# Forget rows' log sums in the gate stage, residual rows one chunk later, and six other moves in a hybrid decoder layer

## Chip, cores and metric

The kernel runs on one core of a Trainium2 chip. Its time is the device time of one execution in microseconds. The core's engines work in parallel, each through its own queue in order: TensorE (PE, with its weight loads PEld), VectorE (DVE), ScalarE (ACT), GpSimd (POOL) and SyncE (SP), which issues most DMAs.

## What is computed

The reference is one decoder layer for 1024 tokens of width 1024, in float32. Cut to what matters:

```python
z = h @ w_in
hq, hf, hi, hg, sq, sk, sv, mq, gl = split_cols(z, IN_SPLITS)
f = lb + (1 - lb) * sigmoid(hf); k = 1 - f
b = cumsum(log f) within chunks of 64 tokens      # gated recurrence, 8 heads
q_in, k_in, k_out = hq * exp(b), k * exp(-b), k * exp(b_last - b)
o_a = rms_norm(recurrence(q_in, k_in, k_out, hi)) * gain * silu(hg)
o_b = sliding_window_attention(sq, sk, sv)        # 16 heads, window 128
o_c = memory_attention(mq, mem @ w_mem_kv)        # 4 heads, 256 memory rows
merged = sum of sigmoid(gl_i) * (o_i @ w_branch_i)
h = layer_norm(alpha * h + merged @ w_out)
h = layer_norm(alpha * h + relu(h @ w_up) ** 2 @ w_down)
```

## The kernel before

A float32 product is made of three matmuls: each operand is split into a high part (float32r, copied by ScalarE, `L76`) and a low part (the difference, on GpSimd or VectorE, `L77`). A weight tile of 128x1024 is loaded into a tile R, and its two parts go to a tile W; both rings have 4 tiles, S has 2, G and T have 4.

Parts of the layer are computed by a scheme with seven block products in place of eight (Strassen's in Winograd's form): `prod(o, w, g, j)` is twelve matmuls of block product j with the operand `xs[j]`, and `combine` makes the operands 3 to 7 from the four blocks of x. The order in time:

- The keys and values of the memory (to 56 us in the profile), which use the S tiles.
- The gate stage: 16 rows (pairs of weight tiles) that need only x: the two other branch gates, the forget gate hf and the output gate hg. `two` makes products 1 and 2 of the first twelve rows ("the firsts"); meanwhile `x_rest(k)`, k = 0 to 3, makes the operands 3 to 7. Then `run` makes products 6, 4, 7, 5 and 3 of each row (3 is put off into the next row); rows 12 to 15 make all seven. `prepare` loads and combines the weights of a row on GpSimd: w2 (products 4 and 5), w4 (6), w3 (7 and 3). `z_emit` and `z_first` pass the sums through Tanh and store them in `d_z`.
- For each half of the tokens: sliding window attention (`swa_phase`), memory attention (`mem_head`), the recurrence (`hg_head`), output projection, LayerNorm. `hg_gates` loads forget rows and makes Ln, running sums (scans) and Exp in the midst of memory attention.
- The up projection, again by block products, whose operands `flip_h1` turns with TensorE and combines; behind it the down projection, in chunks c of 7 products whose partial sums `pa[j]` stay in SBUF; last, the rows of the output, four products each, with LayerNorm (`last_rows`, `norm_rows`).

Tiles come from rings: a new tile waits until the oldest user of its place is done. Engines take their instructions in the order that the tile framework has laid out, which is not always that of the code; so a change of a ring or of the code moves instructions on all engines.

Of the kernel before, what the change touches and what calls it, by code (L numbers as in the profile page):

```python
# [8 lines left out]
F32 = mybir.dt.float32  # L9
# [6 lines left out]
P = 128  # L16
D = 1024
# [18 lines left out]
def hybrid_layer(ctx: ExitStack, tc: tile.TileContext, a: dict, out: bass.AP):  # L36
# [110 lines left out]
    gainh = const("gainh", [P, 8])  # L147
    d_bias = dr.tile([16, 256], F32, name="d_bias")
# [5 lines left out]
    d_z = dr.tile([16, 4, P, TH], F32, name="d_z")  # L154
    d_g1 = dr.tile([EARLY_Z, P, TH], F32, name="d_g1")
# [39 lines left out]
    def combine(left, right, part, eng):  # L195
# [78 lines left out]
    nc.vector.tensor_scalar(out=c1, in0=lb, scalar1=-0.5, scalar2=0.5, op0=ALU.mult, op1=ALU.add)  # L274
    nc.vector.tensor_scalar(out=gainh, in0=gain, scalar1=0.5, scalar2=None, op0=ALU.mult)
# [60 lines left out]
    def prepare(src0, src1, first):  # L336
# [10 lines left out]
        w4 = st("S", [P, 2, TH], F32R)  # L347
        split(w4[:, 0], w4[:, 1], r1[:, H], nc.vector)
# [3 lines left out]
    def run(ws, p1, held, emit):  # L352
# [17 lines left out]
        b_ = pt("t")  # L370
        prod(b_, w2, 0, 5)
# [8 lines left out]
    zrows = [("w_gate", 0), ("w_gate", 16), ("w_hf", 0), ("w_hg", 0)]  # L380
# [6 lines left out]
    def forget(f, h):  # L387
        nc.vector.tensor_scalar(out=f, in0=f, scalar1=1.0, scalar2=c1[:, h:h + 1], op0=ALU.add, op1=ALU.mult)
        nc.vector.tensor_scalar(out=f, in0=f, scalar1=lb[:, h:h + 1], scalar2=None, op0=ALU.add)

    def z_emit(i):
        box = []

        def emit(b, o, s_):
# [4 lines left out]
            if i < 12:  # L399
# [121 lines left out]
    def swa_phase(hf, x, merged, fill_last):  # L521
# [17 lines left out]
        nc.scalar.copy(vt, o)  # L539
# [755 lines left out]
```

## Time and profile before

| | us |
|---|---|
| median of 3 runs (lowest, highest) | 2166.62 (2166.34, 2167.66) |
| profiled execution | 2166.51 |
| its span, first to last instruction | 2164.7 |
| TensorE busy | 2054.9 (95%) |
| VectorE, GpSimd, ScalarE busy | 1252.5, 959.3, 837.7 |

The span is what the profile shows between the first and the last instruction. An engine's busy time counts its instructions and not its waits; TensorE's busy time is longer where the granted clock was lower (mean 0.983 of full speed).

### The profile page before, as it was taken

Reading aid. Unit: us, or ns where it says so; the run is one execution under the profiler, and the core shown is the slowest. Engines: PE = TensorE matmul, PEld = TensorE weight load, DVE = VectorE, ACT = ScalarE, POOL = GpSimd, SP = SyncE. Lnnn points to the kernel's source line nnn. Section 1 sums busy time; section 2 is a strip of 40 time slices with the busy share of each in tenths; the row PEclk is TensorE's granted clock in tenths of the full one; section 3 lists DMA queues with packets and bytes.
Section 4 is the critical chain, followed back from the end, with each engine's and each line's share of the span. In section 5 each row is a group of like instructions: output and inputs, shape, how many; then the busy total and the mean of one; then the engine's idle time right before and its main releaser. Section 6 shows DMA issues by size and latency. Waiting matters only on the chain. (4 is left out here: it accounts for less than half of the span.)

```text
span 2164.7 us, 26923 instructions
## 1 busy us (share of the span) xinstructions
PE 2054.9 (95%) x10050; PEld 1688.5 (78%) x10050; DVE 1252.5 (58%) x2092; ACT 837.7 (39%) x1480; POOL 959.3 (44%) x478
## 2 busy tenths in 40 slices
PE   8969998999999999999999999999899999999996
PEld 8747776777787898877778889887678887788875
DVE  5643276566536346256753624626566656598898
ACT  5423222344335233335433614333544454433322
POOL 2556665421222522751122242274533334777674
PEclk9989999999999999999999999999999999999998
DMA  8653432422233323544123332354657547744322
GB/s 281 215 161 127 155 121 93 145 89 69 60 102 110 124 84 117 177 145 136 59 69 103 102 123 84 121 187 144 199 186 228 182 145 240 275 136 154 116 88 78
DMA packets 125762, 299.30 MB, mean 138 GB/s; under 512 B 11408, under 2 KB 24896, under 8 KB 125632
## 3 DMA queue, kind: packets, MB, share of 16 engines
q1 hardware_dynamic: 124736, 294.42, 41.7%
q10 hardware_dynamic: 896, 3.16, 0.5%
q8 instruction: 79, 1.29, 0.3%
q14 instruction: 51, 0.42, 0.1%
HBM read 232.51 MB, written 65.03 MB: 137 GB/s over the span
## 5 line engine op out<-in xcount | busy, mean ns | idle before, releaser
L77 POOL TENSOR_TENSOR W<-R,W 128x1024 fp32r<-128x1024 f32 x205 | 497.0, 2426 | 879.3 <-ACT W L76 835.1
L61 PE MATMUL pz<-X,W 128*128 128x512 f32 x2016 | 491.9, 398 | 30.5 <-ACT W L76 11.3
L76 ACT CAST W<-R 128x1024 fp32r<-128x1024 f32 (+1 forms) x287 | 293.8, 1024 | 469.5 <-PE pz L61 226.1
L61 PEld LDWEIGHTS pz<-X,W 128*128 128x128 f32 x2016 | 377.7, 191 | 114.4 <-POOL W L77 12.9
L61 PE MATMUL pz<-O,W 128*128 128x512 f32 x1152 | 267.1, 391 | 0.0
L61 PEld LDWEIGHTS pz<-O,W 128*128 128x128 f32 x1152 | 214.9, 188 | 46.2 <-issue 1.5
L61 PE MATMUL pt<-O,W 128*128 128x512 f32 x768 | 188.0, 393 | 2.3 <-DVE T L296 2.3
L61 PEld LDWEIGHTS pt<-O,W 128*128 128x128 f32 x768 | 142.3, 188 | 39.5 <-DVE T L296 10.3
L77 DVE TENSOR_TENSOR W<-R,W 128x1024 fp32r<-128x1024 f32 (+1 forms) x84 | 100.5, 1197 | 75.3 <-ACT W L76 74.9
L61 PE MATMUL pz<-BT,W 128*128 128x512 f32 x384 | 102.1, 419 | 24.8 <-DVE G L315 9.7
L61 PEld LDWEIGHTS pz<-BT,W 128*128 128x128 f32 x384 | 76.4, 203 | 47.6 <-issue 12.7
L61 PE MATMUL ps<-W,BT 128*128 128x512 f32 x360 | 98.4, 391 | 5.3 <-DVE X L296 3.3
L61 PE MATMUL pz<-W,BT 128*128 128x512 f32 x354 | 96.3, 390 | 0.4 <-DVE X L1070 0.4
L61 PE MATMUL pz<-W,X 128*128 128x256 f32 x768 | 95.8, 284 | 0.0
L77 POOL TENSOR_TENSOR BT<-R,BT 128x1024 fp32r<-128x1024 f32 x27 | 72.1, 2671 | 51.4 <-ACT BT L76 51.4
L61 PE MATMUL ps<-X,W 128*128 128x512 f32 x384 | 93.0, 391 | 1.6 <-DVE G L296 1.6
L61 PEld LDWEIGHTS pz<-W,X 128*128 128x128 f32 x768 | 93.1, 192 | 0.0
L61 PE MATMUL ps<-T,W 128*128 128x512 f32 x384 | 92.2, 389 | 0.0
L61 PEld LDWEIGHTS ps<-X,W 128*128 128x128 f32 x384 | 72.6, 189 | 17.5 <-DVE G L296 2.3
L341 POOL TENSOR_TENSOR R<-R,R 128x512 f32<-128x512 f32 x48 | 64.3, 1340 | 48.8 <-DMA R<-in_w_gate_dram 31.1
L61 PEld LDWEIGHTS ps<-T,W 128*128 128x128 f32 x384 | 72.1, 188 | 15.0
L77 POOL TENSOR_TENSOR MG<-R,MG 128x1024 fp32r<-128x1024 f32 (+1 forms) x30 | 79.5, 2651 | 9.0 <-ACT MG L76 9.0
(277 smaller groups left out, 3454.9 us busy)
## 6 DMA issues: line engine op xcount, KB each, us to landing
R<-d_ff SPq DMA_DIRECT2D x49, 512.0 KB, 3.6
R<-in_w_b_dram SPq DMA_DIRECT2D x48, 512.0 KB, 3.5
R<-in_w_up_dram SPq DMA_DIRECT2D x42, 512.0 KB, 4.1
R<-in_w_gate_dram SPq DMA_DIRECT2D x40, 512.0 KB, 3.6
d_ff<-T SPq DMA_DIRECT2D x56, 256.0 KB, 2.8
d_z<-T SPq DMA_DIRECT2D x52, 256.0 KB, 2.0
G<-d_z SPq DMA_DIRECT2D x48, 256.0 KB, 2.8
d_ff<-S SPq DMA_DIRECT2D x48, 256.0 KB, 2.3
```

What stands on the lines that cost most here:

```text
L61: nc.tensor.matmul(o, lhsT=l, rhs=r, start=start, stop=stop, skip_group_check=more)
L76: (hi_copy or nc.scalar.copy)(hi, src)
L77: (lo_eng or nc.gpsimd).tensor_tensor(out=lo, in0=src, in1=f32(hi), op=ALU.subtract)
L341: nc.gpsimd.tensor_tensor(out=o, in0=a_, in1=b_, op=op)
```

## The change

It does eight things. `x_rest` takes its raw tiles from S and not from R, and `prepare(0)` moves behind the firsts; w4 of a row takes a W tile, not S. In the rows with early firsts, products 4 and 5 come ahead of 6 and 7. The rows hf and hg change places, and the forget rows make k = 1 - f, Ln, scans, Exp and the subtraction in the gate stage; k goes to `d_z`, the sums to a new `d_b`, the ends of the chunks stay in `elc`; `hg_gates` only loads. The copy of v in `swa_phase` goes to VectorE. `flip_h1` of half 2 keeps one turned block in PSUM and the left blocks in a tile R; in `combine`, products 6 and 4 change engines. The residual rows are loaded in chunks 1 to 4 of the down projection and added there by five operations of 128x2048. In six of the eight last rows, ScalarE makes sum and squares in place of VectorE's bn_stats.

```diff
@@ x_rest
-            raw = st("R", [P, 2, TH])
+            raw = st("S", [P, 2, TH])
@@ prepare
-        w4 = st("S", [P, 2, TH], F32R)
-        split(w4[:, 0], w4[:, 1], r1[:, H], nc.vector)
+        w4 = st("W", [P, 2, 1024], F32R)
+        split(w4[:, 0, L], w4[:, 1, L], r1[:, H], nc.vector)
@@ combine
-        part(6, b22, 1)
+        part(6, b22, 0)
...
-        part(4, b21, 0)
+        part(4, b21, 1)
@@ run
+        if p1 is not None:
+            c, b_ = four(), five()
         prod(o, w4, 0, 6, p1 is not None)
...
         prod(o, w3, 0, 7, False)
@@ rows
-    zrows = [("w_gate", 0), ("w_gate", 16), ("w_hf", 0), ("w_hg", 0)]
+    zrows = [("w_gate", 0), ("w_gate", 16), ("w_hg", 0), ("w_hf", 0)]
@@ forget, called behind the last addition of rows 12 to 15
+    def forget(i, f, ks):
+        for b in range(4):
+            h = 2 * (i - 12) + b % 2
+            nc.scalar.activation(ks[b // 2][:, b % 2], f[:, b, :], AF.Identity, scale=nc1[:, h:h + 1], bias=c1[:, h:h + 1])
+            nc.sync.dma_start(d_z[i, b], ks[b // 2][:, b % 2])
+            nc.vector.tensor_scalar(out=f[:, b, :], in0=f[:, b, :], scalar1=c1[:, h:h + 1], scalar2=c1b[:, h:h + 1],
+                                    op0=ALU.mult, op1=ALU.add)
+        nc.scalar.activation(f, f, AF.Ln)
+        for b in range(4):
+            nc.vector.tensor_tensor_scan(out=f[:, b, :], data0=reset, data1=f[:, b, :], initial=0.0,
+                                         op0=ALU.mult, op1=ALU.add)
+        h = 2 * (i - 12)
+        nc.scalar.activation(elc[:, h:h + 2, :, :].rearrange("p h f c -> p f h c"),
+                             f.rearrange("p (f h) (c t) -> p f h c t", f=2, t=64)[:, :, :, :, 63], AF.Exp)
+        gp = f.rearrange("p h (c u t) -> p (h c) u t", u=2, t=64)
+        nc.vector.tensor_tensor(out=gp[:, :, 0, :], in0=gp[:, :, 0, :],
+                                in1=gp[:, :, 0, 63:64].broadcast_to([P, 16, 64]), op=ALU.subtract)
+        nc.sync.dma_start(d_b[i - 12].rearrange("b p t -> p b t"), f)
@@ gate stage
-        if i == EARLY_Z - 3:
-            ws = prepare(*zsrc(0), False)
...
-        if i:
-            ws = prepare(*zsrc(i), i >= EARLY_Z)
+        ws = prepare(*zsrc(i), i >= EARLY_Z)
@@ swa_phase
-        nc.scalar.copy(vt, o)
+        nc.vector.tensor_copy(vt, o)
@@ hg_gates (its finish(), with Ln, scans and Exp, is gone)
+        for pp in range(2):
+            i = 2 * b4 + pp
+            nc.sync.dma_start(fk[:, 2 * pp:2 * pp + 2, :], d_z[12 + i, 2 * hf:2 * hf + 2].rearrange("b p t -> p b t"))
+            nc.sync.dma_start(gg[:, 2 * pp:2 * pp + 2, :], d_b[i, 2 * hf:2 * hf + 2].rearrange("b p t -> p b t"))
@@ flip_h1
-            both = st("W", [P, 2, 8, P])
+            left = st("R", [P, 8, P])
...
+                if g == 0:
+                    t = st("G", [P, TH]).rearrange("p (k t) -> p k t", k=4)
+                    nc.scalar.copy(t, o)
+                    o = t
+                right.append(o)
@@ down
-            rows_h1(2, 0, 0)
-            rows_h1(5, 1, 1)
-            rows_h1(3, 0, 1)
-            nc.gpsimd.tensor_tensor(out=pa[3], in0=pa[3], in1=pa[5], op=ALU.subtract)
-            rows_h1(0, 1, 0)
...
-            if c == 0 and j in (2, 3, 5):
-                nc.vector.scalar_tensor_tensor(out=pa[j][:, b, :], in0=pa[j][:, b, :], scalar=ALPHA, in1=o,
-                                               op0=ALU.mult, op1=ALU.add)
+        if 1 <= c <= 4:
+            rows_h1(0, *((1, 0), (0, 0), (0, 1), (1, 1))[c - 1])
...
+                for j, sign in (((4, 1),), ((2, 1),), ((3, 1),), ((5, 1), (3, -1)))[c - 1]:
+                    nc.vector.scalar_tensor_tensor(out=pa[j], in0=pa[0], scalar=sign * ALPHA, in1=pa[j], op0=ALU.mult,
+                                                   op1=ALU.add)
@@ last_rows
+                if own:
+                    nc.vector.bn_stats(out=bn[:, ch, :], in_=v)
+                else:
+                    nc.scalar.activation(st("G", [P, TH]), v, AF.Copy, accum_out=ss[:, ch:ch + 1])
...
+                    nc.scalar.activation(st("G", [P, TH]), parts[ch][0], AF.Square, bias=neg, accum_out=qq[:, ch:ch + 1])
```

How the instructions stand on three engines. GpSimd's queue before, at the end of the firsts: row 34 is the low part of w3 of gate row 0, rows 35 and 36 and rows 39 and 40 begin the combining of rows 1 and 2, rows 37 and 38 are the low parts of the firsts' weights 10 and 11.

```order
34 L77 TENSOR_TENSOR W_1117<-R_1103,W_1117 128x1024 [waits Activation_49]
35 L341 TENSOR_TENSOR R_1264<-R_1264,R_1266 128x512 [waits DMAHW7_49,DMAHW5_49,DVE_49]
36 L341 TENSOR_TENSOR R_1266<-R_1266 128x512 [waits Pool_49]
37 L77 TENSOR_TENSOR W_1122<-R_1120,W_1122 128x1024 [waits DMAHW1_49,Activation_49]
38 L77 TENSOR_TENSOR W_1162<-R_1160,W_1162 128x1024 [waits DMAHW2_49,Activation_49]
39 L341 TENSOR_TENSOR R_1360<-R_1360,R_1362 128x512 [waits DMAHW4_49,DMAHW1_49,Pool_49]
40 L341 TENSOR_TENSOR R_1362<-R_1362 128x512 [waits DMAHW0_49,Pool_49]
41 L77 TENSOR_TENSOR W_1270<-R_1266,W_1270 128x1024 [waits Activation_49]
```

The same place now: rows 28 and 31 are the low parts of weights 10 and 11, rows 30 and 32 the last pieces of x_rest(3), row 34 is w2 of gate row 0, row 38 its w3, and row 33 begins gate row 1.

```order
28 L77 TENSOR_TENSOR W_1111<-R_1109,W_1111 128x1024 [waits Activation_49]
29 L347 TENSOR_TENSOR R_1191<-R_1191 128x512 [waits Pool_49]
30 L77 TENSOR_TENSOR O_116<-S_1051,O_116 128x512 [waits DMAHW1_49,Activation_49]
31 L77 TENSOR_TENSOR W_1151<-R_1149,W_1151 128x1024 [waits Activation_49]
32 L77 TENSOR_TENSOR T_122<-S_1051,T_121 128x512 [waits Activation_49]
33 L347 TENSOR_TENSOR R_1270<-R_1270,R_1272 128x512 [waits DMAHW7_49,DMAHW5_49,Pool_49]
34 L77 TENSOR_TENSOR W_1195<-R_1191,W_1195 128x1024 [waits Activation_49]
35 L347 TENSOR_TENSOR R_1272<-R_1272 128x512 [waits Pool_49]
36 L347 TENSOR_TENSOR R_1191<-R_1191,R_1189 128x512 [waits Pool_49]
37 L347 TENSOR_TENSOR R_1189<-R_1189,R_1191 128x512 [waits Pool_49]
38 L77 TENSOR_TENSOR W_1203<-R_1189,W_1203 128x1024 [waits Activation_49]
39 L347 TENSOR_TENSOR R_1366<-R_1366,R_1368 128x512 [waits DMAHW6_49,DMAHW3_49,DVE_49]
```

So the low parts of the weights 10 and 11 no longer stand behind the combining of gate row 1, but behind x_rest; and the combined weights of row 0 come behind all of it.

VectorE's queue before, between two late gate rows (T_2542 and T_2677 are the sums of two rows; row 225 is a copy that TensorE waits for):

```order
222 L404 SCALAR_TENSOR_TENSOR T_2542<-G_2660,T_2542 128x512 [waits Activation_49]
223 L296 TENSOR_TENSOR T_2677<-ps_2664,G_2645 128x512 [waits DMAHW6_49,DMAHW4_49,DMAHW7_49,DMAHW2_49,PE_49]
224 L404 SCALAR_TENSOR_TENSOR T_2677<-G_2679,T_2677 128x512 [waits Activation_49]
225 L315 COPY G_2695<-pz_2632 128x512 [waits PE_49]
226 L77 TENSOR_TENSOR S_2760<-R_2752,S_2760 128x512 [waits DMAHW5_49,Activation_49]
```

And now (T_2413 is row 12, T_2558 row 13; the rows of L416 are the scans, listed under their opcode's name; row 203 waits for Exp; rows 198 and 204 are copies for TensorE):

```order
198 L321 COPY G_2573<-pz_2494 128x512 [waits PE_49]
199 L416 SCALAR_TENSOR_TENSOR T_2413<-reset,T_2413 128x512 [waits Activation_49]
200 L416 SCALAR_TENSOR_TENSOR T_2413<-reset,T_2413 128x512
201 L416 SCALAR_TENSOR_TENSOR T_2413<-reset,T_2413 128x512 [waits DVE_49]
202 L416 SCALAR_TENSOR_TENSOR T_2413<-reset,T_2413 128x512
203 L422 TENSOR_TENSOR T_2413<-T_2413 128x16x64 [waits Activation_49]
204 L321 COPY G_2600<-pz_2494 128x512 [waits PE_49]
205 L412 TENSOR_SCALAR T_2558<-T_2558,c_76,c1b 128x512 [waits Activation_49]
206 L302 TENSOR_TENSOR T_2558<-ps_2575,G_2600 128x512 [waits DVE_49]
207 L302 TENSOR_TENSOR T_2558<-pt_2604,G_2600 128x512 [waits PE_49]
```

The copy behind product 6 (row 198) is free of the STT; the copy behind product 7 (row 204) now stands behind the scans and the subtraction of the row before.

ScalarE's queue before, at the first flip of the up projection: rows 792 to 798 are the flip's casts, rows 799 and 801 the weights 4 and 5.

```order
792 L76 CAST O_11493<-W_11639 128x4x128 [waits Activation_49]
793 L929 ACTIVATE G_11634<-G_11634 128x512 [waits Activation_49]
794 L76 CAST O_11494<-W_11639 128x4x128 [waits DMAHW4_49,DVE_49]
795 L76 CAST BT_11497<-W_11639 128x4x128 [waits DVE_49]
796 L76 CAST MG_11495<-W_11639 128x4x128 [waits DVE_49]
797 L292 COPY G_11685<-pz_11672 128x512 [waits DMAHW6_49,PE_49]
798 L76 CAST T_11499<-W_11639 128x4x128 [waits DVE_49]
799 L76 CAST W_11775<-R_11773 128x1024 [waits DMAHW2_49,DVE_49,Pool_49]
```

And now: row 802 is weight 5 (weight 4 is row 796), rows 805 to 811 are the flip's casts, two of them from PSUM.

```order
802 L76 CAST W_11824<-R_11822 128x1024 [waits DMAHW1_49,PE_49,Pool_49]
803 L924 COPY G_11656<-pt_11651 128x512 [waits DMAHW2_49,PE_49]
804 L948 ACTIVATE G_11644<-G_11644 128x512 [waits DVE_49]
805 L76 CAST O_11503<-pt_11658 128x4x128 [waits PE_49]
806 L949 ACTIVATE G_11644<-G_11644 128x512 [waits Activation_49]
807 L76 CAST O_11504<-R_11649 128x4x128 [waits DMAHW4_49,DVE_49]
808 L76 CAST BT_11507<-G_11656 128x4x128 [waits DVE_49]
809 L76 CAST MG_11505<-pt_11658 128x4x128 [waits DVE_49]
810 L298 COPY G_11695<-pz_11682 128x512 [waits DVE_49,PE_49]
811 L76 CAST T_11509<-R_11649 128x4x128 [waits DVE_49]
```

Both weights have moved ahead of the flip.

## Rows read from the trace of the kernel before

**Rows 1.** The page: busy time of each engine.

```profile
PE 2054.9 (95%) x10050; PEld 1688.5 (78%) x10050; DVE 1252.5 (58%) x2092; ACT 837.7 (39%) x1480; POOL 959.3 (44%) x478
```

**Rows 2.** What TensorE waits for: microseconds in total, times, the longest.

```profile
PE pz L61 <- POOL W L77: 11.1, 3, 8.8
PE pz L61 <- DVE G L315: 9.7, 3, 3.3
PE ps L61 <- DVE O L99: 5.7, 2, 3.3
PE ps L61 <- ACT BT L98: 4.0, 2, 2.0
```

**Rows 3.** Timeline, TensorE, end of the firsts: start, duration, operation, idle before.

```profile
123.95 1.22 PE L61 MATMUL pz<-X,W 128*128 128x512 f32 x2 [6.75 <-ACT W L76]
133.97 4.64 PE L61 MATMUL pz<-X,W 128*128 128x512 f32 x10 [8.80 <-POOL W L77]
146.90 2.88 PE L61 MATMUL pz<-MG,S 128*128 128x512 f32 x12
```

**Rows 4.** Timeline, VectorE and TensorE, gate row 14, then busy and granted clock.

```profile
388.23 2.41 DVE L404 SCALAR_TENSOR_TENSOR T<-G,T 128x512 f32<-128x512 f32 x1 [3.57 <-ACT G L403]
391.39 4.57 PE L61 MATMUL pz<-BT,W 128*128 128x512 f32 x12 [3.28 <-DVE G L315]
391.50:394.50 3.00, 3.00 (x8) 2.34 (x9) 1.22 (x1) 0.62 (x1) 1.55 (x2) 0.52 0.25 89
```

**Rows 5.** Timeline, VectorE and TensorE, start of half 2.

```profile
963.62 2.14 DVE L1192 TENSOR_TENSOR sm<-sm,sm 128x1 f32<-128x1 f32 x1
968.39 6.88 PE L61 MATMUL pz<-X,W 128*128 128x512 f32 x22 [4.54 <-ACT G L539]
```

**Rows 6.** Timeline, TensorE, up projection.

```profile
1514.23 0.93 PE L61 MATMUL pz<-X,W 128*128 128x512 f32 x2 [4.53 <-ACT W L76]
```

**Rows 7.** Timeline, TensorE, first chunk of the down projection.

```profile
1843.70 2.93 PE L61 MATMUL ps<-W,MG 128*128 128x512 f32 x6 [4.34 <-DVE O L1070]
```

**Rows 8.** Timeline, TensorE's last matmuls and VectorE's last scale.

```profile
2144.30 0.84 PE L61 MATMUL pz<-W,MG 128*128 128x512 f32 x3
2157.92 0.16 DVE L1211 SCALAR_TENSOR_TENSOR sm<-sm,sm 128x1 f32<-128x1 f32 x1
```

**Rows 9.** Timeline, SyncE's queue and VectorE: memory keys' store, loads and end of x_rest.

```profile
65.57 0.33 SPq L253 DMA_DIRECT2D d_mkv<-S  x1
84.06 0.38 SPq L218 DMA_DIRECT2D R<-in_xT_dram  x1
98.82 0.39 SPq L218 DMA_DIRECT2D R<-in_xT_dram  x1
111.45 0.69 DVE L77 TENSOR_TENSOR T<-R,T 128x512 fp32r<-128x512 f32 x1
```

**Rows 10.** Timeline, GpSimd, low parts in the gate loop.

```profile
194.21 2.40 POOL L77 TENSOR_TENSOR W<-R,W 128x1024 fp32r<-128x1024 f32 x1
209.26 2.40 POOL L77 TENSOR_TENSOR W<-R,W 128x1024 fp32r<-128x1024 f32 x1
215.56 2.38 POOL L77 TENSOR_TENSOR W<-R,W 128x1024 fp32r<-128x1024 f32 x1 [1.16 <-ACT W L76]
```

**Rows 11.** Timeline, ScalarE and VectorE, hg_gates of half 1.

```profile
685.08 1.28 ACT L674 ACT_TABLE_LOAD   x1
686.38 1.91 ACT L674 ACTIVATE T<-T 128x2048 f32<-128x2048 f32 x1
659.57 6.34 DVE L677 TENSOR_TENSOR_SCAN T<-reset,T 128x512 f32<-128x512 f32 x4
```

**Rows 12.** VectorE on 128x2048: groups by line, then the timeline.

```profile
L1093 DVE SCALAR_TENSOR_TENSOR X<-X 128x2048 f32<-128x2048 f32 x1 | 2.6, 2567 | 0.0
2096.05 4.49 DVE L296 TENSOR_TENSOR O<-O,O 128x2048 f32<-128x2048 f32 x1
```

**Rows 13.** Stretch of the down projection: busy PE, PEld, DVE, ACT, POOL.

```profile
1880.00:1930.00 50.00, 49.97 (x221) 41.08 (x220) 44.09 (x51) 18.03 (x18) 39.63 (x15) 1.00 0.51 168
```

More of the change, by code (lines that the diff above doesn't have):

```diff
@@ L154, in hybrid_layer @@
     d_z = dr.tile([16, 4, P, TH], F32, name="d_z")
+    d_b = dr.tile([4, 4, P, TH], F32, name="d_b")
     d_g1 = dr.tile([EARLY_Z, P, TH], F32, name="d_g1")
@@ L274, in hybrid_layer @@
     nc.vector.tensor_scalar(out=c1, in0=lb, scalar1=-0.5, scalar2=0.5, op0=ALU.mult, op1=ALU.add)
+    nc.vector.tensor_scalar(out=nc1, in0=c1, scalar1=-1.0, scalar2=None, op0=ALU.mult)
+    nc.vector.tensor_tensor(out=c1b, in0=c1, in1=lb, op=ALU.add)
     nc.vector.tensor_scalar(out=gainh, in0=gain, scalar1=0.5, scalar2=None, op0=ALU.mult)
@@ L362, in run, with four, five @@
             emit(0, d, s1)
+        c, b_ = None, None
+        def four():
+            c_ = pt("s")
+            prod(c_, w2, 1, 4)
+            return c_
+        def five():
+            t = pt("t")
+            prod(t, w2, 0, 5)
+            return t
+        if p1 is not None:
+            c, b_ = four(), five()
         prod(o, w4, 0, 6, p1 is not None)
         s2 = copy_out(o) if p1 is None else plus(o, p1)
-        c = pt("s")
-        prod(c, w2, 1, 4)
+        if p1 is None:
+            c = four()
         prod(o, w3, 0, 7, False)
@@ L369, in run @@
         emit(1, c, s3)
-        b_ = pt("t")
-        prod(b_, w2, 0, 5)
+        if p1 is None:
+            b_ = five()
         emit(3, b_, s3)
@@ L404, in emit @@
                 nc.vector.scalar_tensor_tensor(out=f, in0=th, scalar=1.0, in1=f, op0=ALU.add, op1=ALU.mult)
-            if 8 <= i < 12:
-                forget(f, 2 * (i - 8) + b % 2)
-            nc.sync.dma_start(d_z[i, b], f)
+            if i < 12:
+                nc.sync.dma_start(d_z[i, b], f)
+            elif b == 2:
+                forget(i, box[0], [st("S", [P, 2, TH]) for _ in range(2)])
         return emit
@@ L430, in emit @@
             add(t, o, s_)
-            nc.scalar.activation(t, t, AF.Tanh, scale=0.5)
-            if i >= 8:
-                forget(t, 2 * (i - 8) + b % 2)
+            if i // 4 == 2:
+                u = st("G", [P, TH])
+                nc.scalar.activation(u, t, AF.Tanh, scale=0.5)
+                nc.vector.scalar_tensor_tensor(out=t, in0=u, scalar=1.0, in1=t, op0=ALU.add, op1=ALU.mult)
+            else:
+                nc.scalar.activation(t, t, AF.Tanh, scale=0.5)
             nc.sync.dma_start(d_z[i, b], t)
@@ L800, in hybrid_layer @@
                 hgs = [hg_gates(0, hf)]
-                hgs[0][3]()
         v = keep()
@@ L888, in flip_h1 @@
                 return
-            both = st("W", [P, 2, 8, P])
-            left, right = both[:, 0], both[:, 1]
+            left = st("R", [P, 8, P])
             nc.sync.dma_start(left, d_h1t[:, :, ts])
+            right = []
             for g in range(2):
@@ L1142, in last_rows @@
             bn = sb.tile([P, 4, 6], F32, tag="bn", name=nm("bn"), bufs=8)
+            own = b in (2, 3)
+            ss = small(2)
             parts = []
@@ L1200, in layer_norm, with norm_rows @@
             store(cs, v)
-def norm_rows(nc, small, parts, bn, g, b, eps, mhalf, store, last):
-    mv, e, y, z, nb = small(2), small(1), small(1), small(1), small(1)
-    nc.vector.bn_aggr(out=mv, in_=bn)
+def norm_rows(nc, small, parts, mv, g, b, eps, mhalf, store, last):
+    e, y, z, nb = small(1), small(1), small(1), small(1)
     nc.vector.tensor_scalar(out=e, in0=mv[:, 1:2], scalar1=eps, scalar2=None, op0=ALU.add)
```

77 lines of the change are left out of this document (32 added, 45 removed).

## The prediction

> **What bounds the kernel now.** I read the engine shares first: TensorE is busy for 2054.9 of 2164.7 us [rows 1]. The change leaves the number of matmuls alone, so it can act only on the 110 us in which TensorE stands, and on matmuls at the lower granted clock. Next came the list of what TensorE waits for, then the timeline around each long wait. The waits lie in few places: the gate stage (weights that come late from ScalarE and GpSimd, [rows 2, 3], and copies of VectorE, [rows 2, 4]), the memory attention of both halves (5.7 us behind O of VectorE and 4.0 behind BT of ScalarE, [rows 2]), the start of half 2 [rows 5], of the up projection [rows 6] and of the down projection [rows 7], and the time behind the last matmul [rows 8]. A long wait has a second price: the twelve matmuls behind it take 4.57 us [rows 4] against 2.88 [rows 3], at a granted clock of 0.52, the level of 1.2 GHz [rows 4], so 1.7 us lost. The profiled execution took 2166.51 us, 0.1 below the median of 2166.62; the sum is made against 2166.5.
>
> **Gate start, the largest term.** In the program before, POOL's queue holds the subtraction of gate row 1, which waits for a DMA, ahead of the low parts of weights 10 and 11, so TensorE stood 6.75 and 8.80 us [rows 3] and reached the first product of row 0 at 146.90. Twelve firsts from 56 us need 12 x 5.44 = 65.3 us, so without waits they would end at 121.4. The change orders POOL otherwise, but puts x_rest into the two S tiles. Those belong to the memory keys until the store issued at 65.57 [rows 9] has landed, so the second half of x_rest(0) is issued near 69, my estimate. The chain is as long as before: second halves were issued at 84.06 and 98.82, a cycle of 14.8 us, and the last piece ended at 112.1, 13.3 behind its issue [rows 9]. With two tiles, a load also waits for the chain before it, so I keep 14.8: x_rest(3) is issued near 113.5 and ends near 127. In POOL's new queue the low part of weight 11 stands behind O of x_rest(3) (near 119), so the firsts end near 127, not 121.4. Behind T of x_rest(3) come: sub 1.3, low part of w2(0) 2.4, add 1.3, two subs 2.7, a cast 1.2, low part of w3(0) 2.4, a load 3.7, sub and add 2.6, w2(1) 2.4. That is w2(1) near 147; one POOL row of 15.05 us [rows 10] puts w2(2) at 162 and w2(3) at 177. Before, w2(3) ended at 196.6 [rows 10]: POOL runs 19.5 us earlier.
>
> TensorE does not gain all of it. POOL's row of 15.05 us, against 13.6 us of products, paces the loop before and after; moving products 4 and 5 ahead only moves the short wait that each row has. But the new order places four matmuls of product 4 of row i+1 ahead of product 7 of row i. Before, three products (8.2 us) were left behind the start of w3(11), which is 3.9 us behind the end of w2(11), as in every row [rows 10]; now seven (19.0 us) are left behind w2(11). That costs 19.0 - 12.5 = about 6.5. **Term: -13.** Bounds: if S were free as early as R was, x_rest(3) would end at 112 and the gain be 28; with a cycle 3 us longer it would be 5.
>
> **Late gate rows.** Rows 12 to 15 become the forget rows. Each adds four Identity copies and one Ln of 128x2048 on ScalarE, four small tensor_scalars, four scans and a subtraction on VectorE, five stores. The long ones were measured: Ln 1.91, table load 1.28, scans 6.34 together [rows 11]. They no longer have the STT of 2.41 us ahead of the copy [rows 4], which was behind 9.7 us of waits [rows 2] and three spells of low clock, 14.8 us in all. The new wait: VectorE's subtraction needs ScalarE's Exp, which stands behind a cast that waits for TensorE's product 5. Behind that subtraction stand the copy s3, a tensor_scalar and two additions that TensorE's product 3 needs: four of 0.69 us, as the last row of [rows 9], are 2.8, and 5.7 if those that read SBUF alone are stretched as the STT was. With 2.9 + 1.7 at two borders and 4.4 before the sliding window, where only four matmuls of two weights lie between, the new loss is about 12. **Term: -3** (from -11, all waits gone, to +10).
>
> **Memory attention.** hg_gates now only loads. Gone are the Ln, the scans in front of VectorE's O [rows 11], and the Exp in front of ScalarE's BT: 5.7 + 4.0 + 1.7 = 11.4. I leave 1.9 for new order among the same matmuls; the loads grow from 1 to 2 MB, and VectorE and ScalarE have a whole head's time for them. **Term: -9.5** (-8 to -11).
>
> **Start of half 2.** The copy of v moves from ScalarE, where it stood behind a normalization, to VectorE, behind a small operation that ended at 965.76 [rows 5]; copy 0.69, so TensorE goes on near 966.5 and not 968.39. **Term: -2** (0 to -6 with the clock).
>
> **Up projection.** The turned rows no longer take a weight tile. In ScalarE's new queue the casts of weights 4 and 5 stand ahead of the flip that the cast at the wait of 4.53 us stood behind [rows 6]; that wait goes, and the two behind it that GpSimd ended (2.3, what the list has beside the 8.80, [rows 2]), 6.8 in all, with one spell of 1.7 at least. The waits at row 0 behind them come from GpSimd's low parts, which stay. Cover: two weights (10.9 us of products) between a flip and the weight behind it; a flip's chain took some 7 us. **Term: -8** (-4 to -11).
>
> **Down projection.** The residual leaves chunk 0: no subtraction on GpSimd behind a load, so 4.34 us and the slow matmuls behind it [rows 7] go, and 12 reads of PSUM pass to ScalarE, which is idle half the time. VectorE gets four more STT of 128x2048: 2.57 us each as the one before, 4.49 at worst, as an addition took beside GpSimd [rows 12]. They fall where it is busy 44 of 50 us [rows 13]: one per chunk fits in, two in chunk 4 may not. **Term: -6.5** (-2 to -8.5).
>
> **Last rows.** Two bn_stats per row go from VectorE and four passes with accumulators come to ScalarE, in a loop between both. VectorE ended 12.8 us behind TensorE (2157.92 against 2145.14, [rows 8]). ScalarE has some 5 us of work a row against 5.44 of TensorE, but each row now crosses between the two engines six times. **Term: -0.5** (-4 to +3). Products 6 and 4 changing engines in combine, and the three small constants, cost nothing: VectorE was idle there.
>
> Sum: 13 + 3 + 9.5 + 2 + 8 + 6.5 + 0.5 = 42.5; 2166.5 - 42.5 = **2124**.
>
> **A rule against the change.** In the row, a table load on ScalarE takes 1.28 us, the Ln began 0.02 us behind it [rows 11], and eight loads are made before as after. The Trainium skill (ScalarE: Activation LUTs, "What ACT_TABLE_LOAD costs") says that a switch of sets costs a drain of about 1.38 us besides, 2.66 in all, and to do all of one set before the next; the gate stage now alternates Tanh and Ln in every row. By that rule, counted on the path, the sum would be 2135; the trace shows no such drain, so it has a small chance.
>
> **Rivals.**
> - *Late rows bind* (0.17). VectorE has some 18 us of work in a row of 19 us of products once the scans of 6.34 us are in; if they, not the products, set the row, each row takes 3 to 4 us more than I count: the -3 becomes +11, 2138. For it: the stretched STT of 2.41 us in these rows. Against it: GpSimd has fewer low parts there.
> - *x_rest does not bind* (0.16). If the loads fall in earlier gaps, POOL's loop starts as soon as the weights' tiles are free: -28 in place of -13, 2109. For it: in the loop GpSimd has slack at the start. Against it: the S tiles' store at 65.57.
> - *The drain is real* (0.05): each late row with two switches on the path, 4 x 2 x 1.38 = 11 us, 2135. Against it: the Ln 0.02 us behind its load.
> - *Slower* (0.04). The residual loads stand in SP's queue among the loads of the down operands, each waiting for VectorE's STT on the tile that it refills. If VectorE lags, the queue stands, and TensorE runs out of operands at three refills. Price: SP's wait less the two operand sets in hand. It decides from 14 us per refill, 3 x 14 = 42, the whole gain. Against it: VectorE ends its chunk within 6 us of TensorE.
> - *The gain of the gate start is hidden* (0.10): the loop stays paced by POOL and the late rows wait for weights that GpSimd brings no earlier: the term of 13 falls to 0, 2137.
> - My forecast, with all terms near their values: 0.48, own range 2114 to 2132.
>
> **How the numbers follow.** The time is that of the forecast, 2124. Downwards the range takes in the case of 2109; upwards the late rows with a second term failing, about 2144. That is 2107 to 2144. A measurement of this kernel tells about 0.2% (4.3 us) from nothing. All cases but one are faster by more than that; faster 0.94, same 0.02 (several terms at their worst ends add up to little), slower 0.04.
>
> **What would show it.** Gate start: product 4 of row 0 near 130 instead of the first product at 146.90, no wait of 8.80 us; x_rest(3) ending near 127; a wait of about 1 us ahead of product 4 in each row; w2 rows 15 us apart. Late rows: VectorE's copy waited for once per row, its releaser the subtraction behind Exp. Memory attention, TensorE: no waits behind O and BT. Start of half 2: a wait near 2.7 us. Up projection: no wait between the flips. Down: no wait at 1843, no new ones between 1900 and 2100 of the old time. What would make it wrong: the STTs in chunk 4 holding TensorE, or a tail longer by more than 4 us.

## The result: 1% slower, and the profile after

Forecast 2124 us (2107 to 2144); measured 2189.18 (median of 4 runs, 2185.04 to 2191.78) against 2167.14 of the kernel before beside it. The ratio is 1.0099 (95% interval 1.0082 to 1.0117): slower, on the other side of all that the forecast thought likely. The profiled execution took 2191.78 us. Its page, busy time of each engine (answers to [rows 1]):

```profile
PE 2068.2 (94%) x10050; PEld 1700.8 (78%) x10050; DVE 1236.1 (56%) x2080; ACT 869.0 (40%) x1550; POOL 972.7 (44%) x477
```

TensorE is busy 13.3 us longer with the same 10050 matmuls, so more of them ran at the lower clock (the mean granted clock fell from 0.983 to 0.975); and outside that time it stands 121.6 us where it stood 109.8. What it waits for, in total, times, longest (answers to [rows 2]):

```profile
PE pz L61 <- DVE G L302: 26.7, 13, 3.3
PE pt L61 <- DVE T L302: 15.9, 5, 4.3
PE pt L920 <- DVE R L208: 11.2, 3, 5.7
PE ps L61 <- POOL W L77: 8.4, 2, 6.6
...
PE pz L61 <- ACT O L1227: 2.7, 1, 2.7
PE pt L61 <- DVE X L302: 2.2, 1, 2.2
PE pt L908 <- ACT G L910: 2.1, 1, 2.1
```

The waits behind O of VectorE and BT of ScalarE in memory attention are gone, and those behind GpSimd smaller. Of the 13 waits behind G, eleven are waits of product 7 of rows 0 to 10 behind the sum of product 6 (21.8 us); ten of these are new, while that of row 0 and two in the up projection stood before too. New as well are waits of product 3 behind VectorE's sums, and those of the turns (`L920`). To place them, the matmuls that begin a stage were looked up in both timelines of TensorE. Those of the changed kernel:

```profile
135.16 1.16 PE L61 MATMUL ps<-T,W 128*128 128x512 f32 x4 [0.37 <-DVE G L302]
150.67 1.22 PE L61 MATMUL ps<-T,W 128*128 128x512 f32 x2 [6.63 <-POOL W L77]
154.51 0.79 PE L61 MATMUL pz<-BT,W 128*128 128x512 f32 x1 [2.62 <-DVE G L302]
341.69 0.98 PE L61 MATMUL pz<-BT,W 128*128 128x512 f32 x3
469.55 0.60 PE L594 MATMUL pt<-cst,G 128*128 128x128 f32 x4
986.49 0.70 PE L61 MATMUL pz<-X,W 128*128 128x512 f32 x2 [2.68 <-ACT O L1227]
1527.93 0.88 PE L920 MATMUL pt<-cst,T 128*128 128x128 f32 x4 [4.66 <-DVE R L208]
1560.05 1.09 PE L920 MATMUL pt<-cst,T 128*128 128x128 f32 x4 [5.74 <-DVE R L208]
1842.39 0.39 PE L61 MATMUL pt<-W,MG 128*128 128x512 f32 x1
2160.59 0.84 PE L61 MATMUL pz<-W,MG 128*128 128x512 f32 x3
```

| stage, by its matmuls | before, us | after | change | forecast |
|---|---|---|---|---|
| start to product 7 of gate row 0 | 155.7 | 154.5 | -1.2 | -13 |
| from there to product 7 of row 11 | 163.9 | 187.2 | **+23.3** | in the -13 |
| late rows, to the first turn of the sliding window | 122.7 | 127.8 | +5.1 | -3 |
| memory attention, both halves | 224.5 | 212.6 | -11.9 | -9.5 |
| start of half 2, with the sliding window's start | 244.8 | 243.4 | -1.4 | -2 |
| up projection, from its first turn | 327.5 | 331.5 | +4.0 | -8 |
| down projection, to the last matmul | 320.7 | 319.0 | -1.7 | -6.5 |
| last matmul to the end of the span | 19.6 | 28.4 | **+8.8** | -0.5 |

The row "start of half 2" goes from the end of the first half's memory attention to the first heads of the second half's sliding window. The stages left out take 585.3 us before and 585.4 after. The changes shown add up to +25.0; the spans differ by 25.1.

One early gate row of the changed kernel, all engines (those lines that follow on each other):

```profile
199.79 1.05 ACT L76 CAST W<-R 128x1024 fp32r<-128x1024 f32 x1 [2.59 <-PE pt L61]
200.92 2.40 POOL L77 TENSOR_TENSOR W<-R,W 128x1024 fp32r<-128x1024 f32 x1 [2.49 <-ACT W L76]
201.59 2.88 PE L61 MATMUL pz<-MG,W 128*128 128x512 f32 x12
203.39 2.63 POOL L347 TENSOR_TENSOR R<-R,R 128x512 f32<-128x512 f32 x2
204.71 0.62 ACT L76 CAST W<-R 128x512 fp32r<-128x512 f32 x1 [3.34 <-POOL R L347]
205.36 1.22 DVE L77 TENSOR_TENSOR W<-R,W 128x512 fp32r<-128x512 f32 x1 [4.92 <-ACT W L76]
206.50 0.68 DVE L302 TENSOR_TENSOR G<-pz,G 128x512 f32<-128x512 f32 x1
207.23 3.02 PE L61 MATMUL pz<-BT,W 128*128 128x512 f32 x12 [1.86 <-DVE G L302]
210.09 1.98 PE L61 MATMUL ps<-T,W 128*128 128x512 f32 x8
211.90 5.38 PE L61 MATMUL pt<-O,W 128*128 128x512 f32 x23
213.24 1.29 POOL L347 TENSOR_TENSOR R<-R,R 128x512 f32<-128x512 f32 x1 [3.66 <-DMA R<-in_w_gate_dram]
215.54 1.05 ACT L76 CAST W<-R 128x1024 fp32r<-128x1024 f32 x1 [2.58 <-PE pt L61]
```

Read it as a loop, **loop A**: a chain of steps in which each waits for the one ahead of it and the last sets off the first of the next row, so that its length is the time of a row. ScalarE's cast of the next row's w2 waits for product 3 (its W tile is the one that product 3 frees, since w4 too now takes a tile of that ring). Behind it come w2's low part, a subtraction, cast and low part of w4, and only behind that low part, in VectorE's queue, the sum of product 6 that product 7 waits for (199.79 to 207.23, 7.44 us). Products 7, 4, 5 and 3 then take 8.31 us to the next cast: 15.75 us a row, against 13.6 of products.

There is a second loop, **loop C**, in the line at 213.24: GpSimd's first subtraction for a row waits for a load into the R tile that the last low part of an earlier row has freed, and the queue holds w2's low part of another row behind it. In the kernel before, the steps of this loop follow on each other without a gap and fill the row of 15.05 us [rows 10]; its wait for the load there:

```profile
221.61 1.30 POOL L341 TENSOR_TENSOR R<-R,R 128x512 f32<-128x512 f32 x1 [3.66 <-DMA R<-in_w_gate_dram]
```

The Trainium skill says that the queues of ScalarE, VectorE and GpSimd are strictly first in, first out (PSUM — Partial Sum Buffer, "Engine vs sequencer instructions"); both loops agree with it: the sum of product 6, whose matmuls had ended at 204.5, began at 206.50, when the low part ahead of it was all but done (206.6).

### The profile page after: what moved, and what is told of

Same layout as the page of the kernel before. It is cut to its first block, busy times and chain, and to the rows that moved or that the text cites. A ratio compares the mean times of both kernels' runs of the same rounds, so it can differ in the third digit from the quotient of the medians.

```text
span 2189.8 us, 27001 instructions
## 1 busy us (share of the span) xinstructions
PE 2068.2 (94%) x10050; PEld 1700.8 (78%) x10050; DVE 1236.1 (56%) x2080; ACT 869.0 (40%) x1550; POOL 972.7 (44%) x477
## 5 line engine op out<-in xcount | busy, mean ns | idle before, releaser
L76 ACT CAST W<-R 128x1024 fp32r<-128x1024 f32 (+1 forms) x303 | 303.8, 1003 | 541.7 <-PE pz L61 235.5
L77 DVE TENSOR_TENSOR W<-R,W 128x1024 fp32r<-128x1024 f32 (+1 forms) x100 | 118.9, 1190 | 136.5 <-ACT W L76 136.2
L61 PEld LDWEIGHTS pt<-O,W 128*128 128x128 f32 x768 | 147.4, 194 | 52.6 <-DVE T L302 21.7
L61 PE MATMUL pz<-BT,W 128*128 128x512 f32 x384 | 110.6, 445 | 26.7 <-DVE G L302 26.7
L61 PEld LDWEIGHTS pz<-BT,W 128*128 128x128 f32 x384 | 82.3, 218 | 51.3 <-DVE G L302 27.0
L61 PE MATMUL pz<-MG,W 128*128 128x512 f32 x384 | 93.7, 389 | 0.0
L61 PEld LDWEIGHTS ps<-T,W 128*128 128x128 f32 x384 | 72.8, 190 | 23.3 <-POOL W L77 7.1
L302 DVE TENSOR_TENSOR T<-pt,G 128x512 f32<-128x512 f32 x64 | 43.9, 686 | 80.7 <-PE pt L61 80.7
```

The source lines that it names most:

```text
L61: nc.tensor.matmul(o, lhsT=l, rhs=r, start=start, stop=stop, skip_group_check=more)
L76: (hi_copy or nc.scalar.copy)(hi, src)
L77: (lo_eng or nc.gpsimd).tensor_tensor(out=lo, in0=src, in1=f32(hi), op=ALU.subtract)
L302: nc.vector.tensor_tensor(out=o, in0=a_, in1=b_, op=op)
```

## Experiments

All kernels are the changed one with the edit shown; times are medians, ratios to the kernel before.

**The W ring and the order of products.** Three kernels alter the gate rows; the fourth (e4) the last rows, further down:

```diff
@@ e1_w4s, prepare
-        w4 = st("W", [P, 2, 1024], F32R)
+        w4 = st("W", [P, 2, 1024], F32R) if first else st("S", [P, 2, TH], F32R)
@@ e2_order, run (e3_both: this and the edit above)
-        if p1 is not None:
-            c, b_ = four(), five()
         prod(o, w4, 0, 6, p1 is not None)
...
+        c = four()
         prod(o, w3, 0, 7, False)
...
+        b_ = five()
@@ e4_tail, last_rows
-            own = b in (2, 3)
+            own = True
```

> The changed kernel with one thing undone: the fourth weight of the early gate rows (of product 6) goes back to the two small S tiles, so the ring of four W tiles again serves two weights per row, not three. Theory A (the ring): in the changed kernel the cast of w2 of a row must wait until product 3 of the row before has ended, and cast, subtractions, low parts and the sum on VectorE form a loop of 15.75 us, which a stretch at the lower clock makes 17.4; with the tile given back the waits of 1.9 us behind G of VectorE (10 of them) go, a row takes 13.6 to 15.1 us, and the kernel is 15 to 26 us faster than the changed one: 2163 to 2174 us. Theory B (the order): products 4 and 5 ahead of product 6 make the row late, since VectorE adds p1 to product 6 behind the low part; then the tile changes nothing: 2184 to 2192 us, the ten waits stay.

> The changed kernel with the products of the early gate rows in the old order (6, 4, 7, 5, then 3 of the row before among them), the fourth weight still in the ring of W tiles. Theory A (the ring): the loop only moves: now the cast of the fourth weight waits for product 5 of the row before, directly ahead of product 6 that needs it; 2180 to 2195 us, one wait of 1.5 to 3 us per row. Theory B (the order): the waits behind G go, and the kernel takes 2163 to 2174 us.

> Both undone in the early gate rows: the old order of products and the fourth weight in S tiles; start of the gate stage, late rows and all else as changed. Both theories: the rows run as before the change (15.05 us), 2160 to 2172 us. If A holds, it stands within 5 us of the kernel that gives only the tile back; if the order has a gain of its own (product 4 and 5 ahead give GpSimd more time), that one is faster by more than 5 us. The gate stage's start should then show its own gain: sliding window up to 10 us earlier than in the kernel before.

Measured: e1 2169.59 (1.0019, 1.0007 to 1.003); e2 2156.64 (0.9954, 0.9937 to 0.997); e3 2183.43 (1.0082, 1.0066 to 1.0097). Each edit alone gains, 19.6 and 32.5 us; both together only 5.8. Theory A as stated fails at e2 (the ring is unchanged and the rows are free), theory B at e1, and both at e3. Two queues, which no edit had named, separate short rows from long ones. In GpSimd's, where the rows are short (e1, e2), the first two subtractions for the next row stand behind the low part of w2; in the kernel before, the changed one and e3 they stand ahead of it. That became theory C. In VectorE's, the same division holds: in e1 and e2 the sum of product 6 stands ahead of the next row's low part of w4, in the other three behind it. So these runs can't tell the two queues apart. (In e3 the last three rows take 18.5 to 19.8 us, behind waits of 3.1 to 5.0 us ahead of product 7, where the first eight take 15.0 to 15.5; this was not followed up.)

**The two loops taken apart.** In e6, e8, e9 and e12, `add_manual_dep(a, b)` puts instruction a behind instruction b of the same queue, without a semaphore. In the gate stage of e6, e9 and e12 all other queues hold the same instructions in the same order as in the changed kernel, and in e8 as in e2. e7 moves a load; its queues differ only at the start of the stage:

```diff
@@ e6_queue, prepare (third is the subtraction that makes w4's source)
-        sub(r0[:, L], r0[:, L], r1[:, L])
+        first_sub = sub(r0[:, L], r0[:, L], r1[:, L])
+        if behind:
+            tc.add_manual_dep(getattr(first_sub, "ins", first_sub), behind[-1],
...
+        behind.append(getattr(third, "ins", third).name)
@@ e7_r1s, prepare
-        r1 = load_raw(src1)
+        r1 = load_raw(src1) if first else st("S", [P, 1024])
+        if not first:
+            nc.sync.dma_start(r1, src1)
@@ e8_slowq, prepare (beside e2_order; low holds w2's low part of the row before)
+        second = sub(r1[:, L], r1[:, L], r1[:, H], ALU.add)
+        if low and not first:
+            tc.add_manual_dep(low.pop(), getattr(second, "ins", second).name,
...
@@ e9_sumfirst, prepare (behind holds the sum of product 6; e12_bothq: this and e6_queue)
+        part = nc.vector.tensor_tensor(out=w4[:, 1, L], in0=r1[:, H], in1=f32(w4[:, 0, L]), op=ALU.subtract)
+        if behind:
+            tc.add_manual_dep(getattr(part, "ins", part), behind.pop(),
...
```

> The changed kernel with one thing altered, GpSimd's queue in the early gate rows: the first subtraction for a row, which waits for the row's weights from memory, is put behind the third subtraction of the row before (in the changed kernel it stands two instructions further ahead, before the low part of w2 of the row before). The queues of TensorE, VectorE and ScalarE and the tiles are those of the changed kernel. Theory C (GpSimd's queue): a row's last low part frees the raw tile, the load into it takes 3.7 to 4.0 us, and the subtraction that waits for it holds up the low part of the row before, so load, two subtractions, w2's low part, two subtractions, a cast and w3's low part make a loop of 15.1 us and more; the new order breaks it: rows of 13.6 us, 2155 to 2172 us. Theory A (the ring of W tiles, with the low part of the fourth weight ahead of the sum of the row before in VectorE's queue): product 3, cast of w2, its low part, a subtraction, cast and low part of the fourth weight, the sum, products 7 and 4 and 5 make a loop of 15.75 us that this edit leaves alone: 2184 to 2192 us.

> The changed kernel with one thing altered: the second raw weight of each early gate row is loaded into the two S tiles, which stand idle there, so that loads into the four raw tiles go two rows further ahead. All queues of the engines keep the order of the changed kernel. Theory C (GpSimd's queue waits for the load): without the 3.7 us of waiting for the load GpSimd's row is about 11.5 us, the row falls to the 13.6 us of products, 2155 to 2172 us. Theory A (the ring of W tiles and VectorE's queue): unchanged, 2184 to 2192 us.

> The kernel with the old order of products (which was 32.5 us faster than the changed one), and GpSimd's queue put back: the low part of w2 of an early gate row stands again behind the first two subtractions of the next row. Theory C: the rows fall back to 15.1 us or more, so that 11 rows cost 15 to 25 us: 2171 to 2182 us. Theory A (the ring of W tiles): the ring is the same and the order of products is the same as in the faster kernel, 2152 to 2160 us.

> The changed kernel with one thing altered, VectorE's queue in the early gate rows: the low part of the fourth weight of a row is put behind the sum of product 6 of the row before, which product 7 of that row waits for. The ring of W tiles, the order of products and GpSimd's queue stay as changed. Theory A+C (two loops side by side, each slow enough by itself): loop A (product 3, cast of w2, its low part, cast and low part of the fourth weight, the sum, products 7, 4, 5) is cut, loop C (GpSimd's queue behind the load into the raw tile, 15.1 us) remains: the waits behind G of 1.9 us go, a row takes about 15.1 us and not 17, 2162 to 2173 us. Rival A alone: without loop A the row is that of the products, 13.6 to 14 us, 2150 to 2160 us. Rival: the place of the low part in VectorE's queue does not matter, since the cast of w2 behind product 3 is late in itself: 2182 to 2192 us.

> The changed kernel with both queues of the early gate rows altered, tiles and order of products as changed: GpSimd's first subtraction for a row behind the third of the row before (which alone gained 4 us), and VectorE's low part of the fourth weight behind the sum of product 6 of the row before. Theory A+C: both loops are cut, a row takes the 13.6 to 14.1 us of its products, 2148 to 2160 us, at least 10 us faster than with VectorE's queue alone. Rival A alone: the same as with VectorE's queue alone, within 4 us. Rival (neither queue): 2180 to 2190 us.

Measured: e6 2185.21 (1.0088, 1.0069 to 1.0107), e7 2195.76 (1.0137, 1.0118 to 1.0155), e8 2192.08 (1.0119, 1.0093 to 1.0146), e9 2165.31 (1.0003, 0.9992 to 1.0015), e12 2151.14 (0.9943, 0.9921 to 0.9964). Product 7 in the timelines of TensorE:

| kernel | product 7 of row 0, us | to that of row 11 | on to the sliding window |
|---|---|---|---|
| before / changed | 155.7 / 154.5 | 163.9 / 187.2 | 122.7 / 127.8 |
| e1_w4s | 155.8 | 167.4 | 120.8 |
| e2_order | 150.4 | 155.6 | 123.8 |
| e3_both | 155.3 | 179.0 | 125.6 |
| e6_queue | 146.8 | 186.4 | 127.8 |
| e7_r1s | 160.2 | 184.8 | 126.8 |
| e8_slowq | 153.7 | 191.2 | 125.3 |
| e9_sumfirst | 149.4 | 164.8 | 126.9 |
| e12_bothq | 148.4 | 153.6 | 126.0 |

With GpSimd's queue or the loads freed (e6, e7) the changed kernel's rows stay at 16.9 and 16.8 us: loop A is there. (e7 begins 5.7 us later, and so lies above both forecasts; by the code, its loads wait for S tiles that still belong to x_rest.) With VectorE's queue altered (e9) loop A is cut and the row falls to 15.0 us, which is loop C in plain sight. GpSimd and TensorE in e9:

```profile
234.96 1.28 POOL L350 TENSOR_TENSOR R<-R,R 128x512 f32<-128x512 f32 x1 [4.13 <-DMA R<-in_w_hg_dram]
237.57 2.37 POOL L77 TENSOR_TENSOR W<-R,W 128x1024 fp32r<-128x1024 f32 x1
239.99 0.74 PE L61 MATMUL ps<-T,W 128*128 128x512 f32 x2 [1.49 <-POOL W L77]
240.02 2.66 POOL L350 TENSOR_TENSOR R<-R,R 128x512 f32<-128x512 f32 x2
243.84 2.40 POOL L77 TENSOR_TENSOR W<-R,W 128x1024 fp32r<-128x1024 f32 x1 [1.16 <-ACT W L76]
249.95 1.29 POOL L350 TENSOR_TENSOR R<-R,R 128x512 f32<-128x512 f32 x1 [3.71 <-DMA R<-in_w_hg_dram]
```

The last low part ends at 246.24, the load takes 3.7 us, and 14.99 us pass between the two subtractions. With both queues altered (e12) neither loop is left: 14.0 us a row, 14.2 us less than e9, with the tiles and the order of products of the change. And e8 shows loop C from the other side: the queue put back costs e2 35.4 us. That is more than the 15 to 25 expected; its rows take 17.4 us, and TensorE waits there for product 3's sums and for w4 too, with stretches at the lower clock. What each adds was not taken apart.

**The last rows.** The edit of e4 is shown above.

> The changed kernel with the statistics of all eight last rows on VectorE (bn_stats), none on ScalarE. Theory: the last rows wait in a loop between ScalarE and VectorE of 7.3 us a row against 5.4 of products, which makes the end 8.8 us later behind the last matmul; without it the time from the last matmul to the end falls from 28.4 to about 19.6 us, and the kernel takes 2179 to 2183 us. Rival: the tail is long because VectorE is late with the residual and the sums of products when the last rows begin; then the statistics on VectorE gain under 3 us, 2186 to 2190.

Measured: 2180.38 (1.0066, 1.005 to 1.0083), 8.8 us under the changed kernel; from the last matmul to the span's end 19.6 us again. The theory holds. ScalarE of the changed kernel, two rows:

```profile
2150.33 0.82 ACT L1244 ACTIVATE X<-X,sm,sm 128x512 f32<-128x512 f32 x1 [1.99 <-DVE sm L1242]
2151.76 0.62 ACT L1167 ACTIVATE G<-O 128x512 f32<-128x512 f32 x1
2154.14 0.73 ACT L1178 ACTIVATE G<-X,sm 128x512 f32<-128x512 f32 x1 [1.68 <-DVE sm L1175]
2157.79 0.82 ACT L1244 ACTIVATE X<-X,sm,sm 128x512 f32<-128x512 f32 x1 [1.51 <-DVE sm L1242]
```

7.46 us a row, of which ScalarE waits twice for VectorE (1.68 and 1.51); the sum over the second half of a row (`L1167`) stands behind the scaling (`L1244`) of the row before.

**Start of the up projection.** Two edits: e5 copies the second block, too; e10 puts back the old flips.

```diff
@@ e5_flips, flip_h1
-                if g == 0:
-                    t = st("G", [P, TH]).rearrange("p (k t) -> p k t", k=4)
-                    nc.scalar.copy(t, o)
-                    o = t
-                right.append(o)
+                t = st("G", [P, TH]).rearrange("p (k t) -> p k t", k=4)
+                nc.scalar.copy(t, o)
+                right.append(t)
@@ e10_flipold, flip_h1
-            left = st("R", [P, 8, P])
+            both = st("W", [P, 2, 8, P])
+            left, right = both[:, 0], both[:, 1]
...
```

(The rest of e10 copies both blocks into `right` and makes the parts in the order and on the engines of the kernel before.)

> The changed kernel with the second block of turned rows, too, copied from PSUM into a G tile of its own, so that the two PSUM tiles t are free as soon as ScalarE has copied them. Theory: TensorE's transposes of a flip wait for VectorE's last subtraction on the block in PSUM (4.66, 0.80 and 5.74 us, each with a stretch at the lower clock); with the copy these waits go, up projection 9 to 15 us shorter, 2174 to 2180 us. Rival: VectorE's combine is late in itself, and the wait moves to the products that read what it makes: under 4 us, 2185 to 2190.

> The changed kernel with the edit at the start of the up projection undone: both blocks of turned rows copied by ScalarE into half a W tile, low parts on the engines of the kernel before. Theory: the edit there made that stage 4 us longer (the waits of 4.66, 0.80 and 5.74 us behind VectorE's last reading of the block in PSUM, against 4.53, 1.52 and 0.76 before), so undoing it takes 3 to 6 us off: 2183 to 2187 us, and the transposes wait for nothing. Rival: the 4 us come from VectorE's queue, which now holds other work at that point; then the stage stays as long, 2187 to 2192 us.

Measured: e5 2187.71 (1.0102, 1.0084 to 1.012) and e10 2187.53 (1.0107, 1.0086 to 1.0128); neither differs from the changed kernel by more than the runs scatter. In e5 two of the three waits go and one of 2.75 us is left, but behind the last flip a wait of 12.87 us appears at the products; the stage takes 332.3 us, no less than in the changed kernel (331.5). TensorE and ScalarE of e5:

```profile
1557.30 1.04 ACT L76 CAST W<-R 128x1024 fp32r<-128x1024 f32 x1 [5.70 <-DVE R L302]
1558.78 0.56 ACT L923 COPY G<-pt 128x512 f32<-128x512 f32 x1
1569.65 0.79 PE L61 MATMUL pz<-MG,W 128*128 128x512 f32 x1 [12.87 <-ACT MG L76]
```

The copies of the last turn stand in ScalarE's queue behind a weight's cast that waits 5.70 us: the rival's case. In e10 the stage takes 329.3 us in place of 331.5, and the transposes wait for nothing, but the old waits are back (4.50 behind ScalarE's cast, against 4.53 in [rows 6]). So the edit exchanged one set of waits for another about 2 us dearer; the other half of the 4 us is not explained.

**The parts that gain, together.** Edits of e2, e4, e9 and e10 in one kernel.

> A kernel of the parts that gained: the changed kernel with the old order of products in the early gate rows, VectorE's sum of product 6 ahead of the next row's low part, the statistics of the last rows on VectorE, and the old flips of the up projection. If the parts add up: the kernel with the old order of products (2156.6 us), less 8.8 for the statistics, less 4 for the flips, less 3 to 6 of the wait of 10 us ahead of product 7 of row 0: 2137 to 2142 us. If the statistics and flips only pay beside the waits of the gate stage, which they do not touch, 2148 to 2157 us.

Measured: 2140.1 (six runs; 0.9891, 0.9874 to 0.9908), 24 us faster than the kernel before and 49 than the changed one. The parts add up: beside e2, the start (to product 7 of row 0) is 3.8 us shorter, the up projection 3.2 and the tail 8.8. Its page:

```profile
PE 2048.8 (96%) x10050; PEld 1685.2 (79%) x10050; DVE 1242.4 (58%) x2068; ACT 853.7 (40%) x1506; POOL 977.4 (46%) x477
```

## Why the prediction was wrong, step by step

- **Gate start and early rows (-13, measured +22.1).** The step that failed: "POOL's row of 15.05 us, against 13.6 us of products, paces the loop before and after; moving products 4 and 5 ahead only moves the short wait that each row has." The 15.05 was kept as a fixed pace of GpSimd. It is loop C, with a load in it that the prediction lists and does not see as a wait that the order of a queue makes; it goes when two subtractions move (from 15.0 us in e9 to 14.0 in e12). That w4 takes a third tile of the W ring was costed at nothing, and the queue of VectorE was not read at this place. In the kernel before, the low part of w4 already stood ahead of the sum of product 6 there, and product 7 waited about 1 us a row:

```profile
213.71 1.24 DVE L77 TENSOR_TENSOR S<-R,S 128x512 fp32r<-128x512 f32 x1 [6.05 <-ACT S L76]
215.47 0.68 DVE L296 TENSOR_TENSOR G<-pz,G 128x512 f32<-128x512 f32 x1
216.30 3.01 PE L61 MATMUL pz<-BT,W 128*128 128x512 f32 x12 [0.99 <-ACT T L400]
```

  But then the cast of w2 waited for product 5. Now it waits for product 3, which comes later, and this closes loop A. That VectorE's order is a link of it is shown by e9; that the ring put the cast behind product 3 is read from the tiles and the trace, since no run alters the ring and leaves the queues alone. The first half of the step was near: x_rest(3) ended at 129.0 (127 foretold), w2(0)'s low part at 133.1 (130.7 by the sum), w2(1)'s at 150.6 (147), and product 4 of row 0 began at 135.2 (near 130). But the wait ahead of product 7 grew to 1.86 us, and the lower clock came with it. In e2 this stretch is 13.6 us shorter than before, near the -13; that is luck and no support, since its rows take 14.1 us and the forecast kept them at 15.05. (In the sum, 8.2 + 3.9 is 12.1 and not 12.5, which changes the term by 0.4.)
- **Late rows (-3, +5.1).** The new wait was the one foretold, with its releaser and near its size: product 3 waits 3.8, 3.8 and 3.2 us behind the scans and subtractions of the forget rows, 10.8 in all, where 2.9, 2.9 and 4.4 were counted. VectorE, ScalarE and TensorE around the scans of row 12:

```profile
382.89 8.23 DVE L416 TENSOR_TENSOR_SCAN T<-reset,T 128x512 f32<-128x512 f32 x4 [0.91 <-ACT T L414]
391.21 0.26 ACT L419 ACTIVATE elc<-T 128x32 f32<-128x32 f32 x1 [4.47 <-DVE T L416]
391.50 1.79 DVE L422 TENSOR_TENSOR T<-T 128x1024 f32<-128x1024 f32 x1 [0.38 <-ACT elc L419]
393.21 0.68 DVE L321 COPY G<-pz 128x512 f32<-128x512 f32 x1
395.22 0.68 DVE L302 TENSOR_TENSOR T<-pt,G 128x512 f32<-128x512 f32 x1
395.95 0.79 PE L61 MATMUL pt<-O,W 128*128 128x512 f32 x1 [3.81 <-DVE T L302]
```

  The four scans took 8.23 us and not the 6.34 of [rows 11]; why is not shown. The step that failed is a fourth wait, which the term does not have. It comes before any scan has run: product 3 of row 11 waits for a sum that stands in VectorE's queue behind the low part of w4 of row 12.

```profile
348.37 1.21 DVE L77 TENSOR_TENSOR W<-R,W 128x512 fp32r<-128x512 f32 x1 [6.73 <-ACT W L76]
351.55 5.49 PE L61 MATMUL pt<-O,W 128*128 128x512 f32 x12 [4.32 <-DVE T L302]
```

  This wait (4.3 us) stands in every kernel with the new order of products and w4 in a W tile, and in none with the old order (e2, e3, e8, e11). With the same forget rows, e2 takes 1.1 us more here than the kernel before; so about 4 of the 5.1 us came with the order of products. The prediction's own addition was off too: 2 x (2.9 + 1.7) + 4.4 is 13.6 and not about 12, so that the term would be -1.
- **Memory attention (-9.5, -11.9)** and **start of half 2 (-2, -1.4)** came as told, the first 0.9 us beyond its bound of -11: no waits behind O and BT, and 2.68 us at the start of half 2 where 4.54 stood [rows 5], less a new wait of 2.1 at `L908`.
- **Up projection (-8, +4.0).** The foretold waits went (e10 brings them back). What failed is "Cover: two weights (10.9 us of products) between a flip and the weight behind it": the flip's last reader in PSUM is now VectorE's last subtraction, and the next turn needs that PSUM tile. That is not all of it: with the tile freed (e5) the waits move to the products, and the stage is no shorter.
- **Down projection (-6.5, -1.7).** The wait of 4.34 us [rows 7] went, and 42 us into the stage TensorE was 7.8 us ahead of the kernel before, more than the term. What was mis-sized is the loss behind it, which the term puts near nothing: a wait behind X grew from 0.5 to 2.2 us (at 1888.85, with a granted clock of 0.93 from 1876 to 1900), and waits of 0.7 and 1.4 behind O are new (1992.50 and 2032.33). By the last matmul 6.1 us were lost again. Whether the residual's operations on VectorE cause these waits was not tried.
- **Last rows (-0.5, +8.8).** "Each row now crosses between the two engines six times" stood in the text and was priced by busy time. The waits at the crossings are the price: 7.5 us a row against 5.44. The longer tail was one of the prediction's own signs of being wrong.
- **Rivals.** None was this case. The slower one, SP's queue in the down projection, did not happen: TensorE's longest wait in that stage is one of 3.3 us that stood there before too. The hidden gain of the gate start had the rows still paced by a loop, but priced the term at 0 and not at a loss. The drain is not in this trace either: in row 12 the load of 1.28 us begins at 379.64, right behind the cast that ends at 379.62, and Ln at 380.94, and the Trainium skill's 1.38 us besides (ScalarE: Activation LUTs, "What ACT_TABLE_LOAD costs") are not seen.

## What to carry to other kernels

When a steady loop shows a period, find the chain that closes it (which tile's release, which place in which queue) before costing an edit: here a period of 15.05 us was no engine's pace. An edit that gives a ring one more user per round, or changes the order in one queue, can open one loop and close another. Each early row held two: with one cut, the other still set the row (16.9 us in e6, 15.0 in e9), and only with both cut did it come near its products (14.0 in e12). When work passes to an idle engine, count the crossings on the path and not only the busy time moved: in the last rows they cost 8.8 us.

## What was not expected of the hardware

The short waits cost more than their length in one kernel and nothing more in another. Stretches of the early rows in the changed kernel, with busy PE, PEld, DVE, ACT, POOL, then the granted clock:

```profile
157.00:326.00 169.00, 150.12 (x596) 119.63 (x594) 52.14 (x66) 44.55 (x60) 95.31 (x57) 0.92 0.37 122
225.00:228.00 3.00, 3.00 (x9) 2.33 (x8) 0.56 (x1) 0.00 (x0) 0.32 (x1) 0.55 0.57 168
```

and in e9, with seven waits of 1.0 to 1.9 us:

```profile
157.00:314.00 157.00, 146.53 (x636) 118.17 (x634) 58.36 (x71) 46.29 (x62) 101.04 (x60) 1.00 0.41 142
```

The wait of 1.9 us ahead of product 7 was followed, in most rows, by a stretch at 1.2 GHz (0.55, after TensorE had stood); as loop A runs through those matmuls, the stretch lengthened the row itself, from 15.75 to about 17.4 us. In e9 the clock stayed at 2.4 GHz.
